# One step of a hybrid decoder layer on one core: in the last of a tile's four attention units, one product with a broadcast reciprocal in the place of two scalings by a column

## The chip, the core and the metric

The kernel runs on one core of a Trainium2 chip. The metric is the time of one execution on the device in microseconds (us); several executions of a kernel are measured and their median is given. The engines of the core are called here as the profile calls them: PE is TensorE (matrix products, with PEld for its weight loads), DVE is VectorE, ACT is ScalarE, POOL is GpSimd, and SP is SyncE, which here only issues transfers. Each engine works through its own instructions in the order in which they stand, and waits where a result of another engine is not there yet.

## The reference

One layer is computed for 2048 prompt tokens and 64 sampled tokens of width 1024: a normalised input goes through one projection, whose columns feed two groups of heads, a sliding-window attention and a gated linear attention (GLA); both outputs are joined, projected and added to the input, and a squared-ReLU MLP follows. The change is in the softmax of the sliding-window attention, cut here to what matters:

```python
def sink_softmax(scores, mask, sink):
    scores = jnp.where(mask, scores, -jnp.inf)
    m = jnp.maximum(jnp.max(scores, axis=-1, keepdims=True), sink)
    p = jnp.exp(scores - m)
    return p / (jnp.sum(p, axis=-1, keepdims=True) + jnp.exp(sink - m))

def swa_banded(q, k, v, sinks):
    # blocks of 128 queries, each against its own 128 keys and the 128 before
    ...
    p = sink_softmax(scores, mask, sink)
    out = jnp.einsum('bnhgqk,bnkhd->bnqhgd', p.astype(v.dtype), vv)
```

There are 8 query heads and 2 key heads, each 64 wide. Everything is float32 at the inputs and outputs; the kernel splits each operand of a large matrix product into a rounded high part and a remainder, and multiplies them in three passes.

## The kernel before

The kernel works in stages. The first (some 20 to 320 us of the profile) runs the sliding-window attention over 16 tiles of 128 prompt tokens, and beside it the input projection of later tiles. Then come the GLA with its own projection, the output projection, and the MLP, which takes the larger part of the time and is bound by PE.

**The attention of a tile** is cut into four units, `unit(i, r, jj, mo)` (L456), for tile `i`, key head `r` and pair of query heads `jj`, in the order (0,0), (0,1), (1,0), (1,1). A unit handles two query heads. Its steps, with the names that the profile uses:

- POOL copies the negated sinks into an extra column of the tile `s` (L464).
- PE computes the scores `sc` of both heads (128 queries by 256 keys each; 128 keys in tile 0).
- DVE adds the mask and takes the row minimum, writing `s` and `m` (the custom instruction and its accumulator read).
- ACT takes the exponential of `s` and sums it into `den`, a column for each head.
- DVE inverts `den` (RECIPROCAL, L487) and scales each head's half of `s` by its column of `den` (two TENSOR_SCALAR instructions, L489). `s` and `den` lie in SBUF, in float32.
- PE transposes the four 128x128 blocks of `s` into `pT`; ACT copies them rounded into `ph`; DVE takes the remainder `pl`.
- PE multiplies with the values into `av`, ACT copies one half to `rest`, and DVE adds both halves into `mo`.

Four units are in flight at different steps, so the engines find work of several units, of the projection (`proj`) and of the next tiles' preparation between them: the transposed input `xT`, split by ACT and DVE into `xh` and `xl`; and the transposed queries and keys `pq` and `pk`, split into `qh`, `ql`, `kh`, `kl` (L406).

**The rotary embedding** of a later tile runs on POOL (`rotate`, L379): two products into `tb` (L386, 320 elements per partition each), one product in place (L392), and two sums into `rot` (L395 with 512 and L401 with 128 elements). All of them read two operands from SBUF. Around them stand small copies on POOL: `kl` (L445, L440), `kh` (L435, L439) and the sinks (L464). In some tiles POOL also multiplies and splits weights of the GLA projection (L261, L263).

**What sets the order.** PE, ACT and DVE instructions of this stage go through `InOrder` (L120), which keeps the order in which the Python code issues them; POOL's and SP's are placed by the scheduler. In every tile, the scaling of unit (1,1) stands on DVE behind the split `qh` and that unit's reciprocal, and ahead of `mo`, the splits of `vv` and `glr`, and the mask step of the next tile's unit. As PE, ACT and DVE are called through this helper, their instructions of the stage carry the line L130 in the profile, and are told apart by the tiles that they write.

Of the kernel before, what the change touches and what calls it, by code (L numbers as in the profile page):

```python
# [16 lines left out]
ALU = mybir.AluOpType  # L17
# [4 lines left out]
P = 128  # L22
# [93 lines left out]
def f32(ap):  # L116
    return ap.bitcast(F32)
# [23 lines left out]
def hybrid_step_kernel(ctx: ExitStack, tc: tile.TileContext, I, O):  # L141
# [21 lines left out]
    te, ac, dv = (InOrder(tc, engine) for engine in (nc.tensor, nc.scalar, nc.vector))  # L163
# [4 lines left out]
    def bank(shape, kind, name):  # L168

        return ps.tile(shape, F32, tag=kind, name=name, bufs=1 if kind in "de" else 2)  # L170
# [285 lines left out]
    def unit(i, r, jj, mo):  # L456

        nkt = min(i + 1, 2)
        nk = nkt * P
        rr = half_of[r]  # L460
        u_ = f"{i}_{r}_{jj}"
        h0 = r * 4 + jj * 2
        s = sp.tile([P, 2, nk + 1], F32, tag="s", name=f"s_{u_}", bufs=3)
        nc.gpsimd.tensor_copy(s[:, :, nk : nk + 1], sink[:, h0 : h0 + 2].unsqueeze(2))  # L464
        yield
        qs, ks, kl = heads[i]
        kh, kl = (t[:, r].rearrange("p a k -> p (a k)")[:, 2 * P - nk :] for t in (ks, kl))
        sc = bank([P, 2, nk], "b", f"sc_{u_}")
        for u in range(2):
            j = jj * 2 + u  # L470
            te.matmul(sc[:, u, :], qs[r][:, j, :], kh, start=True, stop=False)
            te.matmul(sc[:, u, :], qs[r][:, j, :], kl, start=False, stop=True)
        yield
        m = sp.tile([P, 2], F32, tag="m", name=f"m_{u_}", bufs=3)
        for u in range(2):
            dv.tensor_tensor_reduce(
                s[:, u, :nk], sc[:, u, :], amask[:, 2 * P - nk :], scale=1.0,
                scalar=sink[:, h0 + u : h0 + u + 1], op0=ALU.add, op1=ALU.min, accum_out=m[:, u : u + 1],
            )
        yield  # L480
        den = sp.tile([P, 2], F32, tag="den", name=f"den_{u_}", bufs=3)
        for u in range(2):
            ac.activation(
                s[:, u, :], s[:, u, :], AF.Exp, scale=-1.0, bias=m[:, u : u + 1], accum_out=den[:, u : u + 1]
            )
        yield
        dv.reciprocal(den, den)  # L487
        for u in range(2):
            dv.tensor_scalar(s[:, u, :nk], s[:, u, :nk], den[:, u : u + 1], None, op0=ALU.mult)  # L489
        yield  # L490
        pT = bank([P, nkt, 2, P], "c", f"pT_{u_}")
        for u in range(2):
            for kt in range(nkt):
                te.transpose(pT[:, kt, u, :], s[:, u, kt * P : (kt + 1) * P], ident)
        yield
        ph = sp.tile([P, nkt, 2 * P], F32R, tag="ph", name=f"ph_{u_}", bufs=2)
        pl = sp.tile([P, nkt, 2 * P], F32R, tag="pl", name=f"pl_{u_}", bufs=2)
        pf = pT.rearrange("p k u q -> p k (u q)")
        ac.activation(ph, pf, AF.Copy)
        yield  # L500
        dv.tensor_tensor(pl, pf, f32(ph), op=ALU.subtract)
        yield
        av = bank([P, 2 * P], "e", f"av_{u_}")
        vs = [vals[t] for t in range(i + 1 - nkt, i + 1)]
        both, hi, lo = ([v[:, r, u] for v in vs] for u in (slice(2), 0, 1))
        both = [v.rearrange("p u d -> p (u d)") for v in both]
        out = mo[rr, jj * 2 : jj * 2 + 2].rearrange("p j q -> p (j q)")
        if nkt == 1:
            te.matmul(av[:HD], hi[0], ph[:, 0], start=True, stop=False)
            te.matmul(av[:HD], hi[0], pl[:, 0], start=False, stop=False)  # L510
            te.matmul(av[:HD], lo[0], ph[:, 0], start=False, stop=True)
            yield
            ac.activation(out, av[:HD], AF.Copy)
        else:
            te.matmul(av, both[0], ph[:, 0], start=True, stop=False)
            for kt in range(2):
                te.matmul(av[:HD], hi[kt], pl[:, kt], start=False, stop=False)
            te.matmul(av, both[1], ph[:, 1], start=False, stop=True)
            yield
            rest = sp.tile([P, 2 * P], F32, tag="spc", name=f"rest_{u_}", bufs=2)  # L520
            ac.activation(rest[:HD], av[HD:], AF.Copy)
            yield
            dv.tensor_tensor(out, av[:HD], rest[:HD], op=ALU.add)
        if (r, jj) == (1, 1):
            stores.append((mix_d[i][:, 0:4, :], mo))
        yield
# [240 lines left out]
    def units():  # L767
        for i in range(NB):
            mo = sp.tile([P, 4, P], F32, tag="mo", name=f"mo_{i}", bufs=2)
            for u in range(4):  # L770
                yield unit(i, u // 2, u % 2, mo)
        mo = sp.tile([P, 4, NS], F32, tag="mo", name="mo_s", bufs=2)
        for c in range(2):
            for r in range(2):
                yield sample_unit(c, r, cached, kcs, mo)
# [1312 lines left out]
```

## Time and profile before

| | |
|---|---|
| time, median of 3 runs | 2264.04 us (2259.86 to 2265.18) |
| the profiled execution's own time | 2263.19 us |
| its span, first to last instruction | 2261.4 us |
| PE busy | 2183.5 us (97% of the span), 11816 matrix products |
| DVE busy | 1529.9 us (68%) |
| ACT busy | 1221.4 us (54%) |
| POOL busy | 259.4 us (11%), nearly all in the first third |
| granted TensorE clock, mean | 0.995 |

A row of the timeline gives the start and the duration in us, the engine, the line, the operation, the tiles written and read, their shapes, and how many instructions of a kind are merged into the row (xN); a bracket at its end tells how long the engine had been idle before it and what it waited for. A row of the chain of waits gives the start, the length and the holder of one piece of the work that ended last. As instructions of one engine overlap a little in the records, the start of a row can lie a little ahead of the end of the one before it.

### The profile page before, as it was taken

To read this page: it belongs to the slowest core of one execution; us is meant where nothing else is said; L and a number is where in the kernel's file an instruction comes from. 1 tells how busy PE (TensorE), PEld (TensorE's weight loads), DVE (VectorE), ACT (ScalarE), POOL (GpSimd) and SP (SyncE) were. 2 spreads that over 40 slices of the span, in tenths; PEclk is the share of its full clock that TensorE was granted. 3 is DMA by queue.
4 is the path that set the end of the run, shared out by engine and by line. 5 is a ranking of instruction groups with operands and counts; after the bars stand their busy time and mean duration, and the time that the engine had idled before them with its cause. 6 is when DMAs were issued, how large, how long until landed. Compare 5 with 4: busy or idle time off the path is not lost.

```text
span 2261.4 us, 34140 instructions
## 1 busy us (share of the span) xinstructions
PE 2183.5 (97%) x11816; PEld 1868.7 (83%) x11816; DVE 1529.9 (68%) x3102; ACT 1221.4 (54%) x2594; POOL 259.4 (11%) x417
## 2 busy tenths in 40 slices
PE   8999999999999999999999999999999999999998
PEld 7888888999998887788888788887888888788876
DVE  5888877776765565777788664447676666455566
ACT  5778766556664444555545564334544454454444
POOL 3566422111111110000000000000000000000000
PEclk9999999999999999999999999999999999999999
DMA  6334322214335558967777885557644443766675
GB/s 231 119 133 143 102 90 82 67 57 148 126 122 196 184 181 312 313 222 243 251 254 253 284 290 181 180 167 231 195 179 154 154 154 140 252 201 198 192 241 169
DMA packets 237256, 417.81 MB, mean 185 GB/s; under 512 B 25172, under 2 KB 137276, under 8 KB 232972
## 3 DMA queue, kind: packets, MB, share of 16 engines
q1 hardware_dynamic: 237084, 415.64, 54.8%
q8 instruction: 93, 1.52, 0.3%
q14 instruction: 79, 0.65, 0.1%
HBM read 268.44 MB, written 148.18 MB: 184 GB/s over the span
## 4 chain that ended last, share of the span: by engine, by line
PE 64%; DVE 15%; ACT 8%; DMA 8%; issue 3%; POOL 1%; SPq 0%; DVEq 0%; ACTq 0%; POOLq 0%
PE dn L130 21%; PE uc L130 6%; PE ua L130 6%; PE out L1250 6%; PE gproj L130 5%; PE ud L130 3%; PE ue L130 3%; PE ub L130 3%; DMA rt<-t_d 3%; DVE s L130 2%; PE proj L130 2%; PE dsam L130 1%; DVE pl L130 1%; PE o L130 1%; PE sam L130 1%
## 5 line engine op out<-in xcount | busy, mean ns | idle before, releaser
L130 PE MATMUL dn<-o0t,o0s 128*128 128x512 f32 x896 | 350.7, 391 | 9.0 <-ACT o0t L218 8.8
L130 PE MATMUL dn<-o1t,o0s 128*128 128x512 f32 x896 | 351.3, 392 | 3.1 <-DVE o1t L219 3.1
L130 PE MATMUL dn<-o0t,o1s 128*128 128x512 f32 x896 | 349.9, 391 | 0.0
L219 DVE TENSOR_TENSOR o1s<-rs,o0s 128x512 fp32r<-128x512 f32 x224 | 154.6, 691 | 197.2 <-ACT o0s L218 182.8
L218 ACT ACTIVATE o0s<-rs 128x512 fp32r<-128x512 f32 x224 | 141.1, 630 | 249.9 <-PE dn L130 206.0
L130 PE MATMUL gproj<-wg,gx 128*128 128x384 f32 x1408 | 268.5, 343 | 0.1
L130 PEld LDWEIGHTS gproj<-wg,gx 128*128 128x128 f32 x1408 | 241.6, 189 | 4.5 <-issue 4.3
L130 ACT ACTIVATE st<-st 128x512 f32<-128x512 f32 x224 | 141.1, 630 | 158.9 <-DVE st L130 154.9
L130 PEld LDWEIGHTS dn<-o0t,o0s 128*128 128x128 f32 x896 | 168.6, 188 | 48.9 <-ACT o0t L218 11.9
L130 PEld LDWEIGHTS dn<-o1t,o0s 128*128 128x128 f32 x896 | 168.5, 188 | 43.7 <-DVE o1t L219 7.9
L130 PEld LDWEIGHTS dn<-o0t,o1s 128*128 128x128 f32 x896 | 168.5, 188 | 35.0
L219 DVE TENSOR_TENSOR o1t<-rt,o0t 128x512 fp32r<-128x512 f32 x224 | 153.9, 687 | 64.3 <-ACT o0t L218 63.9
L218 ACT ACTIVATE o0t<-rt 128x512 fp32r<-128x512 f32 x224 | 139.6, 624 | 91.7 <-DMA rt<-t_d 70.0
L130 PE MATMUL uc<-H,s 128*128 128x512 f32 x768 | 186.7, 391 | 0.0
L130 PE MATMUL ua<-H,w 128*128 128x512 f32 x744 | 179.2, 390 | 0.0
L130 PEld LDWEIGHTS uc<-H,s 128*128 128x128 f32 x768 | 144.1, 188 | 31.9
L130 PEld LDWEIGHTS ua<-H,w 128*128 128x128 f32 x744 | 138.7, 188 | 28.2
L1250 PE MATMUL out<-wo,mt 128*128 128x512 f32 x680 | 158.9, 392 | 1.9 <-ACT mt L218 1.8
L1250 PEld LDWEIGHTS out<-wo,mt 128*128 128x128 f32 x680 | 126.5, 188 | 28.6 <-ACT mt L218 2.1
L208 POOL TENSOR_TENSOR frs<-rs_v,half 128x1 f32<-128x1 f32 (+1 forms) x13 | 8.4, 657 | 1230.2 <-DVE rs_v L206 1230.2
L130 DVE TENSOR_TENSOR st<-st 128x512 f32<-128x512 f32 x160 | 110.7, 692 | 35.1 <-ACT st L130 31.8
L130 ACT ACTIVATE s<-t 128x1024 fp32r<-128x1024 f32 x62 | 65.8, 1061 | 93.5 <-PE ud L130 29.0
(388 smaller groups left out, 4231.2 us busy)
## 6 DMA issues: line engine op xcount, KB each, us to landing
s_d<-st SPq DMA_DIRECT2D x32, 1792.0 KB, 7.6
rs<-s_d SPq DMA_DIRECT2D x224, 256.0 KB, 2.9
raw<-in_w_up SPq DMA_DIRECT2D x64, 512.0 KB, 5.2
rt<-t_d SPq DMA_DIRECT2D x128, 256.0 KB, 3.3
rt<-in_w_down SPq DMA_DIRECT2D x96, 256.0 KB, 2.8
t<-in_w_down SPq DMA_DIRECT2D x64, 256.0 KB, 3.7
t_d<-t SPq DMA_DIRECT2D x32, 512.0 KB, 6.6
gx<-xt_d SPq DMA_DIRECT2D x28, 512.0 KB, 4.8
```

Source lines behind the costliest of these rows:

```text
L130: ins = call(*a, **k)
L208: nc.gpsimd.tensor_tensor(out, v[:n], e, op=ALU.pow)
L218: nc.scalar.activation(hi, src, AF.Copy)
L219: vector.tensor_tensor(lo, src, f32(hi), op=ALU.subtract)
L1250: te.matmul(banks[c], x, w[:, c * 512 : (c + 1) * 512], start=k + u == 0, stop=k == KT - 1 and u == len(products) - 1,)
```

## The change

In the last of a tile's four units, (r, jj) = (1, 1), the two TENSOR_SCALAR instructions are replaced by one TENSOR_TENSOR product over both heads. Its second operand is `den`, broadcast along the keys (each of its two columns is read 256 times, or 128 times in tile 0). The other three units stay as they were. Each element is multiplied by the same factor as before.

```diff
         dv.reciprocal(den, den)
-        for u in range(2):
-            dv.tensor_scalar(s[:, u, :nk], s[:, u, :nk], den[:, u : u + 1], None, op0=ALU.mult)
+        if (r, jj) == (1, 1):
+            dv.tensor_tensor(
+                s[:, :, :nk], s[:, :, :nk], den.unsqueeze(2).to_broadcast([P, 2, nk]), op=ALU.mult
+            )
+        else:
+            for u in range(2):
+                dv.tensor_scalar(s[:, u, :nk], s[:, u, :nk], den[:, u : u + 1], None, op0=ALU.mult)
         yield
```

In the built program, 32 TENSOR_SCALAR instructions give way to 16 TENSOR_TENSOR instructions at the same places on DVE. Every other instruction of every engine stands where it stood.

## The prediction

> **What bounds the kernel now.** The page has PE busy for 97% of the span, so an edit on DVE can pay only where PE waits. I therefore read the busy time by stage first. The row of the attention stage (its window, the length, then busy time and instructions of PE, PEld, DVE, ACT and POOL, the granted clock, the DMA share and GB/s):
>
> ```profile
> 53.00:300.00 247.00, 231.81 (x1524) 212.15 (x1525) 214.51 (x630) 188.91 (x520) 143.12 (x256) 1.00 0.36 124
> ```
>
> PE is busy 231.81 of 247 us at the full clock: 15 us of waits lie here, and the change is in this stage alone. Next the chain of waits over one tile of it, from one scaling of unit (1,1) to the next:
>
> ```profile
> 141.56 1.51 DVE s L130 x2
> ...
> 145.79 0.69 DVE ql L130
> ...
> 159.07 1.51 DVE s L130 x2
> ```
>
> The chain runs on DVE alone from the first row past `ql` to the splits of the next tile, then over PE and ACT, and back to the scaling. A tile takes 159.07 - 141.56 = 17.51 us, and the 1.51 us pair that the change replaces is a link of this loop. Why 1.51? The timeline of DVE and POOL, in windows so narrow that single instructions show:
>
> ```profile
> 141.56 0.64 DVE L130 TENSOR_SCALAR s<-s,den 128x256 f32<-128x256 f32 x1
> 142.12 0.95 DVE L130 TENSOR_SCALAR s<-s,den 128x256 f32<-128x256 f32 x1
> 141.18 0.87 POOL L386 TENSOR_TENSOR tb<-qk,rope 128x320 f32<-128x320 f32 x1
> 142.01 0.91 POOL L386 TENSOR_TENSOR tb<-qk,rope 128x320 f32<-128x320 f32 x1
> ```
>
> The first scaling ends at 142.20, 0.15 after the first rotary product (142.05); the second at 143.07, 0.15 after the second (142.92). Each waits out one POOL instruction and needs 0.15 us more. Where in the stage does this recur? Three rows of DVE's timeline, for the tiles 0, 14 and 15:
>
> ```profile
> 53.02 1.56 DVE L130 TENSOR_SCALAR s<-s,den 128x128 f32<-128x128 f32 x2
> 298.01 1.44 DVE L130 TENSOR_SCALAR s<-s,den 128x256 f32<-128x256 f32 x2
> 314.29 0.62 DVE L130 TENSOR_SCALAR s<-s,den 128x256 f32<-128x256 f32 x2
> ```
>
> The first two are the first and the last of 15 such collisions, one in each tile. In tile 15 POOL rotates nothing any more, and the pair takes 0.62: its undisturbed price.
>
> **The change part by part.** *The product by itself.* The trace has a product of that size, both operands in SBUF and one of them broadcast, in the GLA stage:
>
> ```profile
> L1118 DVE TENSOR_TENSOR qd<-qz,dec 128x512 f32<-128x512 f32 x14 | 9.6, 686 | 0.0
> ```
>
> 0.69 us against 0.62: where POOL is idle, the change costs 0.07. (The Trainium skill, "VectorE: DVE Perf Modes", section "The perf-mode tier table", speaks against the change in the same way: a float32 scaling out of SBUF runs at the double rate, a two-tensor product at the single one. By that rule alone 16 units would cost 16 x 0.07 = 1.1 us. The trace agrees on the undisturbed prices, but not that they decide, since the pair takes 1.51 here.)
>
> *Does the product wait for POOL too?* Products with both operands in SBUF do, in the GLA stage:
>
> ```profile
> 372.37 1.29 POOL L959 TENSOR_TENSOR s_sg<-s_sg,gp_s 64x512 f32<-64x512 f32 x1 [7.23 <-ACT s_sg L958]
> 373.74 1.27 POOL L961 TENSOR_TENSOR s_sg<-s_sg,ggla 64x512 f32<-64x512 f32 x1
> 372.66 1.15 DVE L1014 TENSOR_TENSOR after<-after,before 128x128 f32<-128x128 f32 x1
> 373.85 1.31 DVE L1015 TENSOR_TENSOR before<-before 128x128 f32<-128x128 f32 x1
> 509.90 1.29 POOL L959 TENSOR_TENSOR sg<-sg,gp 128x512 f32<-128x512 f32 x1 [5.12 <-ACT sg L958]
> 511.27 1.35 POOL L961 TENSOR_TENSOR sg<-sg,ggla 128x512 f32<-128x512 f32 x1
> 510.74 0.73 DVE L1026 SCALAR_TENSOR_TENSOR pr<-gp 128x256 f32<-128x256 f32 x1 [1.05 <-ACT gp L613]
> ```
>
> L1014 ends at 373.81, 0.15 after L959 (373.66), so it got in ahead of the L961 behind it. L1015, issued just after L961 began, sits that one out and ends at 375.16, 0.15 after it. L1026, twice as long, ends 0.28 after its POOL product (511.47 against 511.19). So what is left after the release is about 0.13 us per 128 elements, 0.55 for 512 (an estimate from these rows; its upper bound is the full 0.69 of L1118). The new product is issued at 141.56 as the pair is now, waits until 142.05, gets in ahead of the second rotary product as the first scaling does today, and ends at 142.60. On DVE that gains 143.07 - 142.60 = 0.47 us: one wait in the place of two.
>
> *What POOL pays.* The second rotary product must let the new one pass. Behind today's 0.15 us it took 0.91 instead of 0.87, and L961 behind a pass of 0.28 took 1.35 instead of 1.27 above. So the delay is at least this 0.04 and at most the whole pass of 0.55. I take 0.40, near the upper end, since a pass of 0.15 already costs something and the rest should count in full. POOL's next instructions move by it:
>
> ```profile
> 144.63 1.29 POOL L395 TENSOR_TENSOR rot<-qk,tb 128x512 f32<-128x512 f32 x1
> 145.88 0.46 POOL L401 TENSOR_TENSOR rot<-qk,tb 128x128 f32<-128x128 f32 x1
> 146.88 0.44 POOL L440 CAST kl<-kl 128x256 fp32r<-128x256 f32 x1
> 148.23 0.19 POOL L464 COPY s<-sink 128x2 f32<-128x2 f32 x1 [0.91 <-ACT wg L130]
> ```
>
> *Does the gain pass on?* PE transposes `s` in two steps today, the first as soon as one head is scaled. Afterwards all four blocks wait for the product.
>
> ```profile
> 143.21 0.41 PE L130 MATMUL pT<-ident,s 128*128 128x128 f32 x2 [0.46 <-DVE s L130]
> 143.38 0.43 PE L130 MATMUL proj<-wa_hi,xl 128*128 128x392 f32 x1
> 146.54 0.42 PEld L130 LDWEIGHTS xT<-ident,x 128*128 128x128 f32 x4 [0.45 <-DVE ql L130]
> 147.50 0.60 PE L130 MATMUL pT<-ident,s 128*128 128x128 f32 x4
> 147.86 0.42 PE L130 MATMUL proj<-wa_hi,xh 128*128 128x392 f32 x1
> 143.72 0.60 ACT L130 ACTIVATE ph<-pT 128x512 fp32r<-128x512 f32 x1 [1.23 <-PE pT L130]
> 144.75 0.68 DVE L130 TENSOR_TENSOR pl<-pT,ph 128x512 fp32r<-128x512 f32 x1
> ```
>
> Today the second step starts 0.14 after the scaling, so `pT` would start at 142.74. Four in a row let `proj` start 0.36 later (147.50 to 147.86), at 143.10 instead of 143.38: PE gains only 0.28 here. But it idles 0.45 us before `xT`, where it waits for `ql` on DVE, and the missing 0.19 fits into that. `pT` ends at 143.34 and `ph`, 0.10 later as now, runs to 144.04, ahead of `pl` (144.28 by DVE's own pace). So nothing holds DVE up, and `ql`, `xT` and what follows start 0.47 earlier.
>
> *The next pair*, of unit (0,0), is issued at 146.72 today and ends 0.16 after L440, at 147.48. It moves to 146.25. There the delayed L395 ends at 146.32 and the delayed L401 at 146.74, with 0.04 for letting a scaling in at 146.78, so its second scaling ends at 146.93, 0.55 earlier: by the phase slightly more than 0.47. POOL ends L440 near 147.73, and the sink copy of the last row can still start near 147.76, 0.47 earlier than now; what follows it is not on the chain. I take 0.55 a tile.
>
> *The sum.* Twelve tiles (1, 2 and 4 to 13) at 0.55 give 6.6. Three others differ:
>
> ```profile
> 57.41 0.91 DVE L130 TENSOR_SCALAR s<-s,den 128x256 f32<-128x256 f32 x2
> 110.20 0.43 POOL L440 CAST kl<-kl 128x256 fp32r<-128x256 f32 x1
> 111.54 0.19 POOL L464 COPY s<-sink 128x2 f32<-128x2 f32 x1 [0.90 <-PE pT L130]
> 112.54 0.53 ACT L130 ACTIVATE wg<-wg_raw 128x384 fp32r<-128x384 f32 x1 [1.40 <-POOL wg_raw L261]
> 302.26 0.46 POOL L401 TENSOR_TENSOR rot<-qk,tb 64x128 f32<-64x128 f32 x1
> 302.85 0.65 DVE L130 TENSOR_SCALAR s<-s,den 128x256 f32<-128x256 f32 x2
> ```
>
> In tile 3 the sink copy is followed by weight products that ACT waits for; with L440 ending some 0.45 later, near 111.08, the copy starts near 111.12: 0.42. In tile 0 the pair at 57.41 already waits for POOL's `rot`, which comes no earlier: 0. In tile 14 the pair that ends at 303.50 moves to 302.38 and meets L401, delayed to 302.66 to 303.12, so it ends near 303.26: 0.24. Tile 15 loses 0.07. Together 6.6 + 0.42 + 0 + 0.24 - 0.07 = 7.2 us. Behind the attention only the start moves. The profiled execution goes from 2263.19 (its span of 2261.4 and 1.8 around it) to 2256.0; it lies 0.85 under the median of 2264.04, so against the median the forecast is **2256.8 us**.
>
> **The rivals.** (a) *The product does not wait for POOL.* It ends at 141.56 + 0.69 = 142.25, the tile gains 0.82, 14 tiles 11.5 and tile 0 some 0.6: 2252. For it: `pl` above, a product too, takes 0.68 beside a busy L395. Against it: `pl` reads one operand from PSUM; L1014 and L1015 read both from SBUF and wait.
>
> (b) *PE or POOL sets the pace.* If only PE's 0.28 passes on: 14 x 0.28 = 3.9, so 2260. For it: POOL's slack is nearly used up. Against it: the 0.45 idle before `xT`.
>
> (c) *The second rotary product goes first.* The new product waits until 142.92 and ends at 143.47, 0.40 later than the pair today; 14 tiles make 5.6: 2269.6, slower than before. It decides from the point at which POOL's second product, queued without a gap (142.01 against 142.05), takes its turn ahead of the waiting DVE instruction. Against it: the first scaling wins that turn today. (The Trainium skill, "SBUF — State Buffer", section "Who interferes with whom", has issue order decide, with the loser blocked for the whole instruction; by that the product, issued first, goes first and the sum is the forecast's. L1014 at 0.15 and L1015 at 0.15 after their POOL products agree.)
>
> (d) *It waits for a run of POOL instructions*, through the rotation's third product as well:
>
> ```profile
> 142.99 1.56 POOL L392 TENSOR_TENSOR qk<-qk,rope 128x640 f32<-128x640 f32 x1
> ```
>
> That one ends at 144.55, so the product would end at 145.1, 2.0 later than now, 28 us in 14 tiles: 2292. No row shows a DVE instruction passed over twice.
>
> **How the numbers follow.** Forecast 0.72, (a) 0.10, (b) 0.06, (c) 0.06, (d) 0.06. A measurement here tells 0.3% (6.8 us, the line at 2257.2) from no change. The forecast lies just past that line, and the runs of before spread over 5.3 us, so it falls short of it in some 28 of 100 cases. Faster: 0.72 x 0.72 + 0.10 = 0.62. Within 0.3%: 0.20 + 0.06 + 0.06 = 0.32, with (b) and (c). Slower: (d), 0.06. The forecast's own range, 0.3 to 0.75 a tile, is 2253.5 to 2260.5; with (a), (b) and the spread of the runs it becomes 2251 to 2264.
>
> **What would show it.** Right: unit (1,1)'s scaling as one TENSOR_TENSOR of some 1.05 us that ends 0.55 after the first L386; a second L386 of some 1.3; tiles of 16.95 us; the GLA stage starting some 7 us earlier, all later stages as long as before. A product of 0.69 beside L386 means (a), one of 1.9 means (c), an L386 pair still at 1.74 means that POOL pays nothing. The prediction is wrong if the product shortens as told and the tile keeps its 17.5 us: then another loop over PE, ACT or POOL is as long as this one.

## The result, and the profile after

| | before | the change |
|---|---|---|
| median (runs) | 2262.2 us (20 runs, 2257.31 to 2265.35) | 2256.9 us (20 runs, 2250.69 to 2262.71) |
| ratio to before, 95% interval | | 0.9977 (0.9968 to 0.9985) |
| span of the profiled execution | 2261.4 us | 2251.9 us |
| granted clock | 0.995 | 0.993 |
| first to last scaling of unit (1,1) | 53.02 to 314.29: 261.27 us | 53.11 to 309.33: 256.22 us |

The change is faster by 5.3 us, or 0.23%, with an interval of 0.15 to 0.32%. The forecast of 2256.8 stands beside a median of 2256.9, but that is luck: it was counted from a median of three runs of before, 1.8 us above the one of twenty, and the forecast gain was 7.2 us, 1.9 more than the measured one. The two errors cancel. The same kernel measured again later gave 2255.76 against 2261.2, ratio 0.9977 (0.9967 to 0.9987). The gain is real, as both intervals lie below 1, and most probably a little smaller than the 0.3% that was set as the line between faster and no change. The prediction had given 0.62 to a gain past that line and 0.32 to a time within it; what came is within it.

The two spans differ by 9.5 us, but from the first to the last scaling of unit (1,1) the difference is 5.05. The rest lies in stages that hold the same instructions in both kernels, and is spread from one execution to the next: from the start of the last scaling to the end it is 1947.1 us in before and 1942.6 in the change, and between 1941.7 (e8) and 1947.6 (e11) in the profiles of the experiments below. I therefore read tiles rather than spans.

The chain of waits of the change, one tile (start, length, holder):

```profile
157.00 1.04 DVE s L130
...
160.76 0.69 DVE ql L130
...
161.68 0.10 DVE s L130
161.78 0.49 issue
162.27 0.34 DVE s L130
...
174.20 1.04 DVE s L130
```

The link of 1.51 us is now one of 1.04, and the tile takes 174.20 - 157.00 = 17.20 us in the place of 17.51. The chain runs through the same work as before. The product and its neighbours on POOL, from the timeline of the change in narrow windows, first in this tile, then in tiles 14 and 15:

```profile
157.00 1.04 DVE L130 TENSOR_TENSOR s<-s,den 128x512 f32<-128x512 f32 x1
156.62 2.14 POOL L386 TENSOR_TENSOR tb<-qk,rope 128x320 f32<-128x320 f32 x2
156.62 0.87 POOL L386 TENSOR_TENSOR tb<-qk,rope 128x320 f32<-128x320 f32 x1
157.45 1.31 POOL L386 TENSOR_TENSOR tb<-qk,rope 128x320 f32<-128x320 f32 x1
...
293.23 0.97 DVE L130 TENSOR_TENSOR s<-s,den 128x512 f32<-128x512 f32 x1
309.33 0.69 DVE L130 TENSOR_TENSOR s<-s,den 128x512 f32<-128x512 f32 x1
```

The second L386 starts at 157.45 and takes 1.31 us in the place of 0.91. The product gets in ahead of it and ends at 158.04, 0.55 after the first L386 (156.62 + 0.87 = 157.49). In tile 15, where POOL rotates nothing, the product takes 0.69.

The surprise lies in unit (0,0), whose two scalings were not touched. In the kernel before, its pair took 0.76, in the prediction's tile:

```profile
146.72 0.76 DVE L130 TENSOR_SCALAR s<-s,den 128x256 f32<-128x256 f32 x2
```

Two tiles of the change, the first the one above, the second tile 5:

```profile
161.68 0.67 DVE L130 TENSOR_SCALAR s<-s,den 128x256 f32<-128x256 f32 x1
161.68 0.93 DVE L130 TENSOR_SCALAR s<-s,den 128x256 f32<-128x256 f32 x2
160.49 1.30 POOL L395 TENSOR_TENSOR rot<-qk,tb 128x512 f32<-128x512 f32 x1
161.73 0.47 POOL L401 TENSOR_TENSOR rot<-qk,tb 128x128 f32<-128x128 f32 x1
...
127.39 0.35 DVE L130 TENSOR_SCALAR s<-s,den 128x256 f32<-128x256 f32 x1
127.39 0.82 DVE L130 TENSOR_SCALAR s<-s,den 128x256 f32<-128x256 f32 x2
126.20 1.29 POOL L395 TENSOR_TENSOR rot<-qk,tb 128x512 f32<-128x512 f32 x1
127.44 0.62 POOL L401 TENSOR_TENSOR rot<-qk,tb 128x128 f32<-128x128 f32 x1
```

In both tiles the pair is issued some 0.10 us before L395 ends (161.68 against 161.79, 127.39 against 127.49). In tile 5 the first scaling gets in between L395 and L401 and ends at 127.74, 0.25 after L395. L401 is stretched from 0.46 to 0.62, and the pair takes 0.82. In the other tile the first scaling is passed over: it ends at 162.35, 0.15 after the end of L401 at 162.20, and the pair takes 0.93.

PE behind the product, from the timeline of the change:

```profile
158.18 0.63 PE L130 MATMUL pT<-ident,s 128*128 128x128 f32 x4 [0.56 <-DVE s L130]
158.56 0.43 PE L130 MATMUL proj<-wa_hi,xl 128*128 128x392 f32 x1
```

`pT` starts 0.14 after the product's end, and `proj` 0.38 after `pT`. What PE waits for in this stage, all tiles together (us in total, times, longest), in the kernel before:

```profile
PE pT L130 <- DVE s L130: 8.5, 23, 0.5
```

And in the change, with the busy time of the stage (columns as in the first row of the prediction) behind it:

```profile
PE pT L130 <- DVE s L130: 7.6, 14, 0.6
```

```profile
53.00:300.00 247.00, 233.71 (x1555) 217.66 (x1556) 214.60 (x631) 192.50 (x529) 154.08 (x261) 1.00 0.37 124
```

The waits are fewer, but 7.6 us remain: half a microsecond a tile is left on this path. In the same 247 us PE has 233.71 us of work where it had 231.81, and POOL is busy 154.08 where it was 143.12: the longer second L386 makes 14 x 0.40 = 5.6 of that. The rest is smaller: five more of POOL's instructions fall into the window (261 against 256), since the tiles come earlier, and others, L401 among them, take longer.

### The profile page after: what moved, and what is told of

It reads as the page before. It is cut to its first block, busy times and chain, and to the rows that moved or that the text cites. A ratio compares the mean times of both kernels' runs of the same rounds, so it can differ in the third digit from the quotient of the medians.

```text
span 2251.9 us, 34109 instructions
## 1 busy us (share of the span) xinstructions
PE 2182.2 (97%) x11816; PEld 1872.9 (83%) x11816; DVE 1526.4 (68%) x3086; ACT 1222.8 (54%) x2594; POOL 266.8 (12%) x417
## 4 chain that ended last, share of the span: by engine, by line
PE 71%; DVE 12%; ACT 7%; DMA 6%; issue 2%; POOL 1%; SPq 0%; DVEq 0%; ACTq 0%; POOLq 0%
PE dn L130 23%; PE uc L130 7%; PE ua L130 7%; PE out L1255 6%; PE gproj L130 5%; PE ue L130 4%; PE ub L130 4%; PE ud L130 4%; PE proj L130 2%; DMA rt<-t_d 2%; DVE s L130 2%; PE sam L130 1%; PE dsam L130 1%; PE o L130 1%; DVE pl L130 1%
```

## The experiments

Eleven runs; all but the repetition are variants of the kernel before. Times are medians, ratios are to before in the same comparison.

| run | what differs from before | time | ratio (95%) | (1,1) | (0,0) | tile |
|---|---|---|---|---|---|---|
| e1 | (1,1) product, reciprocal in the score bank | 2251.43 | 0.9951 (0.9939 to 0.9964) | 0.69 | 0.62 | 16.88 |
| e2 | e1, and (0,0) likewise | 2252.94 | 0.9955 (0.9943 to 0.9968) | 0.69 | 0.69 | 16.88 |
| e3 | (1,1) as two products, SBUF | 2267.85 | 1.0024 (1.0015 to 1.0033) | 1.77 | 0.76 | 17.77 |
| e4 | the change, (0,0) product with score bank | 2251.74 | 0.9953 (0.9939 to 0.9966) | 1.03 | 0.69 | 16.97 |
| e5 | (1,1) product, reciprocal in an `av` bank | 2258.98 | 0.9989 (0.998 to 0.9998) | 0.69 | 0.92 | 17.41 |
| e6 | e5, and (0,0) likewise | 2261.43 | 1.0006 (0.9997 to 1.0014) | 0.69 | 0.69 | 17.45 |
| e7 | (1,1) product, reciprocal in the `pT` bank | 2248.65 | 0.994 (0.9928 to 0.9952) | 0.69 | 0.82 | 16.63 |
| e8 | e7, and (0,0) likewise | 2243.06 | 0.992 (0.9907 to 0.9934) | 0.69 | 0.69 | 16.50 |
| e9 | the change again | 2255.76 | 0.9977 (0.9967 to 0.9987) | 1.03 | 0.92 | 17.20 |
| e10 | pairs kept, their reciprocal in the `pT` bank | 2261.3 | 0.9998 (0.9989 to 1.0006) | 1.61 | 0.76 | 17.51 |
| e11 | the change, (0,0) likewise, SBUF | 2252.8 | 0.9972 (0.9961 to 0.9982) | 1.03 | 0.69 | 16.97 |

The last three columns are us in most of the tiles 4 to 11 of the profiled execution: the duration of the scaling in the two units, and the length of a tile.

**Is it the wait for POOL? (e1, e2)** The product stays, its reciprocal is written to PSUM, so that only one of the two operands lies in SBUF; the bank is that of the unit's own scores, which are used up by then (the edit against the change, in unit (1,1)).

```diff
-            dv.reciprocal(den, den)
+            rec = sc[:, 0, :2]
+            dv.reciprocal(rec, den)
             dv.tensor_tensor(
-                s[:, :, :nk], s[:, :, :nk], den.unsqueeze(2).to_broadcast([P, 2, nk]), op=ALU.mult
+                s[:, :, :nk], s[:, :, :nk], rec.unsqueeze(2).to_broadcast([P, 2, nk]), op=ALU.mult
             )
```

Expected of e1, and of e2, which does the same in unit (0,0):

> Unit (1,1) scaled by one product as in the change, but the reciprocal of den is written to the used-up score bank in PSUM, so that the product reads only one operand from SBUF. Theory (a product waits for POOL only where both operands lie in SBUF; the price is the turn that it must wait for): the product takes 0.69 us instead of 1.03, ends 0.82 earlier than the pair of before, the two L386 go back from 2.14 to 1.75 us, a tile takes 16.6 to 16.8 us instead of 17.20 (the change) and 17.51 (before), the time is some 11 us under before, near 2251. Rival (the gain of the change is that of one instruction fewer, wherever den lies): product 1.03, L386 2.14, tile 17.2, time as with the change, 2257.

> As before this one, and unit (0,0) is scaled in the same way, by one product with the reciprocal in PSUM. Theory: neither unit waits for POOL any more, both products take 0.69 us, a tile takes 16.5 to 16.65 us, the time is some 13 us under before, near 2249. Rival (by then another loop, over PE or ACT, is as long as DVE's): the products take 0.69 but the tile stays at 16.7 or more.

DVE, POOL and PE of e1 in one tile:

```profile
171.72 0.69 DVE L130 TENSOR_TENSOR s<-s,sc 128x512 f32<-128x512 f32 x1
171.46 1.69 POOL L386 TENSOR_TENSOR tb<-qk,rope 128x320 f32<-128x320 f32 x2
172.56 0.35 PE L130 MATMUL sc<-kh,qh 128*128 128x256 f32 x1 [0.91 <-DVE s L130]
```

And PE's waits over the stage of e1:

```profile
PE sc L130 <- DVE s L130: 13.4, 15, 1.0
```

The product takes its undisturbed 0.69 in the middle of the L386 pair, and POOL pays nothing (1.69). The wait for POOL was the price, and an operand in PSUM takes it away. The tile of 16.88 is worse than expected: the rows of PE have the reason, a new wait. The next scores need the bank, and PE now waits for the product's end to get it (13.4 us in 15 waits over the stage). In e2 the same wait (13.3 us in 15) holds the tile at 16.88, where 16.5 to 16.65 was expected, so a better (0,0) brings nothing; 16.7 or more is what the rival of that expectation had.

**One instruction or two? (e3)** The scalings of unit (1,1) become two products, a head each, both operands in SBUF (the edit against before, in that unit).

```diff
-            dv.tensor_scalar(s[:, u, :nk], s[:, u, :nk], den[:, u : u + 1], None, op0=ALU.mult)
+            dv.tensor_tensor(s[:, u, :nk], s[:, u, :nk], den[:, u : u + 1].to_broadcast([P, nk]), op=ALU.mult)
```

> Unit (1,1) scaled by two products, one for each head, both operands in SBUF. Theory (each instruction pays a turn behind POOL, and a product's pass is twice as long as a scaling's): the first ends 0.28 after the first L386, the second 0.28 after the second L386, which is itself some 0.15 later: together near 1.8 us instead of 1.51, tile 17.6 to 17.8 us, time 2 to 5 us over before. Rival (a product gets past POOL more easily than a scaling, whatever their number): together 1.2 us or less, tile 17.3 or less, time under before.

The timelines of DVE and POOL in e3:

```profile
162.08 0.77 DVE L130 TENSOR_TENSOR s<-s,den 128x256 f32<-128x256 f32 x1
162.77 1.08 DVE L130 TENSOR_TENSOR s<-s,den 128x256 f32<-128x256 f32 x1
161.70 0.87 POOL L386 TENSOR_TENSOR tb<-qk,rope 128x320 f32<-128x320 f32 x1
162.52 1.04 POOL L386 TENSOR_TENSOR tb<-qk,rope 128x320 f32<-128x320 f32 x1
```

Each waits one POOL instruction out and ends some 0.28 after it: 1.77 together, a tile of 17.77, and the kernel is 0.24% slower than before. That is 6.0 us, more than the 2 to 5 expected; tile 0, which takes 18.57 where it took 16.88, makes 1.7 of it. The product as an operation brings nothing; one turn in the place of two is what pays.

**Is unit (0,0) what is missing? (e4, e11)** Both keep the change in (1,1). e4 takes (0,0) off POOL by the score bank, e11 scales it by a product in SBUF as well. The edit of e4 against the change:

```diff
-        dv.reciprocal(den, den)
-        if (r, jj) == (1, 1):
+        rec = sc[:, 0, :2] if (r, jj) == (0, 0) else den
+        dv.reciprocal(rec, den)
+        if r == jj:
             dv.tensor_tensor(
-                s[:, :, :nk], s[:, :, :nk], den.unsqueeze(2).to_broadcast([P, 2, nk]), op=ALU.mult
+                s[:, :, :nk], s[:, :, :nk], rec.unsqueeze(2).to_broadcast([P, 2, nk]), op=ALU.mult
             )
```

In e11 only the condition changes, to `r == jj`, and `den` serves both units.

> The change as it is for unit (1,1), and unit (0,0) scaled by one product with the reciprocal in PSUM. Theory (the 0.25 us a tile that the change did not bring are spent by the pair of unit (0,0) behind L395 and L401): the product of (1,1) keeps 1.03, that of (0,0) takes 0.69 instead of 0.93, a tile takes 16.95 us instead of 17.20, the time is some 7.5 us under before, near 2254.5. Rival (PE's two-step transposes, or POOL's lateness, hold the tile up): tile 17.2, time as with the change, 2257.

> The change as it is (reciprocal in SBUF), done in unit (0,0) too. By the rule that a product in SBUF waits one POOL instruction out and then needs 0.55 us: in (0,0) it is issued a little before L395 ends and ends 0.55 after L395 if it wins that turn, or 0.55 after L401 if it loses it, as the first scaling does in most tiles of the change. Won: some 0.7 to 0.75 us in (0,0), tile 16.95 to 17.05, time 2250 to 2254. Lost: 0.10 + 0.45 + 0.55 = 1.1 us, tile 17.35 to 17.45, time 2258 to 2260.

Unit (0,0) in e11, on DVE and POOL:

```profile
161.31 0.69 DVE L130 TENSOR_TENSOR s<-s,den 128x512 f32<-128x512 f32 x1
160.13 1.28 POOL L395 TENSOR_TENSOR rot<-qk,tb 128x512 f32<-128x512 f32 x1
161.38 0.95 POOL L401 TENSOR_TENSOR rot<-qk,tb 128x128 f32<-128x128 f32 x1
```

With a (0,0) of 0.69 us the tile is 16.97 in both, the forecast's 16.95, while (1,1) still takes 1.03. So the missing part of a tile's gain lay in unit (0,0) and nowhere else. (The time of e4, 10.1 us under before, is better than the 7.5 expected of it; why is not known. That of e11, 7.8 under before, is as expected.) In e11 the product is issued 0.10 before L395 ends, as the scalings are, but it won that turn in all tiles from 2 to 13: it delays L401 to 0.95 and ends 0.59 after L395.

**Another bank (e5, e6).** The reciprocal goes to an unused half of the previous unit's `av` bank, to avoid the wait of the next scores; in e5 for (1,1), in e6 for (0,0) too.

```diff
-        av = bank([P, 2 * P], "e", f"av_{u_}")
+        avs.append(bank([P, 4 * P], "e", f"av_{u_}"))
+        av = avs[-1][:, : 2 * P]
...
+            rec = avs[-1][:, 2 * P : 2 * P + 2]
+            dv.reciprocal(rec, den)
```

> Unit (1,1) scaled by one product with the reciprocal in PSUM, now in the unused half of the bank of the previous unit's av instead of the score bank, which PE was waiting for. Theory (the tile of 16.88 us of the two kernels with the score bank was held up by PE's 0.91 us wait for that bank): no such wait, product 0.69, L386 pair some 1.7, a tile of 16.7 to 16.8 us with the pair of (0,0) waiting for L401, time near 2250. Rival (with the product at 0.69 another loop of PE or ACT is the bound at 16.88): tile 16.88, time 2251 to 2252.

> As the one before, and unit (0,0) in the same way. Theory: both products take 0.69 us and wait for nothing, a tile takes 16.6 us, the time is near 2248.5, the lowest of all. Rival (another loop is the bound): tile as in the run before, time as there.

Both missed. The product takes 0.69, but the reciprocal ahead of it now waits (e5, timeline of DVE):

```profile
193.85 0.17 DVE L130 RECIPROCAL av<-den 128x2 f32<-128x2 f32 x1 [0.59 <-ACT rest L130]
194.06 0.69 DVE L130 TENSOR_TENSOR s<-s,av 128x512 f32<-128x512 f32 x1
```

ACT reads the other half of that bank for `rest`, and the write waits for it. One wait has been traded for another, and the tile is 17.41.

**A bank that nobody needs meanwhile (e7, e8, e9).** The bank for this unit's own `pT` is taken a step earlier, and the reciprocal lies in its first two columns. PE's transposes into it need the finished product anyway. e7 does it for (1,1), e8 for (0,0) too.

```diff
+        pT = bank([P, nkt, 2, P], "c", f"pT_{u_}")
...
+            rec = pT[:, 0, 0, :2]
+            dv.reciprocal(rec, den)
...
         yield
-        pT = bank([P, nkt, 2, P], "c", f"pT_{u_}")
```

> The product of unit (1,1) with its reciprocal in the bank of this unit's own pT, which PE does not write before the product has ended, and which the softmax leaves alone otherwise. My theory (only a product with both operands in SBUF takes turns with POOL; the 0.36 us a tile that the version with the reciprocal in the score bank lost went to PE's wait for that bank): product 0.69 us, the pair of L386 near 1.69, no wait of the next unit's sc for the product, tiles of 16.6 to 16.8 us instead of 16.88, time 2248 to 2251. Rival: the next loop (ql, xT, the pair of unit (0,0)) is the limit at 16.88 whatever the bank: then the tile stays at 16.9 and the time at that of the score-bank version, 2251 to 2252, and the wait of sc is only replaced by another.

> The same with the product in unit (0,0) too. My theory: both products 0.69 us; the pair of unit (0,0) that this replaces was 0.62 where the first product already stood off POOL, so nothing more is gained unless the pair meets L395 or L401 again at its new place: tiles equal to those of the version with (1,1) alone if its pair is 0.62, up to 0.25 shorter if it is 0.93; time 2247 to 2251. Rival: as there, 16.9 a tile and 2251 to 2252.

> The change itself, beside the two versions above on one chip: 2255 to 2258, tiles of 17.20 us by my theory (the pair of unit (0,0) still loses its turn at the end of L395 in most tiles). Should the tiles be 16.95 this time, the lost turn was an accident of one execution and not of the kernel.

e7 came out as expected: 2248.65, tiles of 16.63 where (0,0) takes 0.82. e9 repeats the change; the first scaling of (0,0) loses its turn again in more than half of the tiles. e8 is better than its expectation by 4 us: 2243.06, in the same comparison 12.7 us below the change and 18.1 below before. Its unit (0,0) on DVE and POOL, then the waits of PE for the transposes and the busy time of its stage (columns as before):

```profile
157.21 0.69 DVE L130 TENSOR_TENSOR s<-s,pT 128x512 f32<-128x512 f32 x1
156.04 1.28 POOL L395 TENSOR_TENSOR rot<-qk,tb 128x512 f32<-128x512 f32 x1
157.28 0.46 POOL L401 TENSOR_TENSOR rot<-qk,tb 128x128 f32<-128x128 f32 x1
```

```profile
PE pT L130 <- DVE s L130: 0.5, 1, 0.5
```

```profile
52.50:299.50 247.00, 241.97 (x1615) 226.20 (x1616) 212.80 (x639) 199.34 (x550) 146.66 (x261) 1.00 0.38 128
```

DVE and POOL work side by side at full pace. PE waits for `s` once in the place of 23 times, and is busy for 241.97 of 247 us where it was 231.81: the stage is now nearly bound by PE. From the first to the last scaling of (1,1) e8 takes 247.03 us, 14.24 less than before, and its first scaling comes 0.55 earlier. The median gains 18.1, and the ratio's interval begins at 0.66%, or 14.9 us; the attention stage does not account for the rest, and single executions differ by up to 6 us behind it.

**The operation or the operand? (e10)** The pairs of scalings stay, their column moves into the `pT` bank.

> In units (0,0) and (1,1) the two scalings stay as before, and only their reciprocal column moves into the bank of pT. This parts the operand's place from the operation. My theory is that what takes turns with POOL is an operation whose large operands both lie in SBUF, or that runs at the double rate; a column of two numbers in PSUM changes neither for the scalings: pair of (1,1) still about 1.5 us, tile 17.4 to 17.6 us, time within 0.2% of before (2258 to 2264). Rival: any operand in PSUM frees an instruction: then each scaling takes 0.35 to 0.42 us beside POOL, the pair of (1,1) 0.65 to 0.75, the tile some 16.5 us, and the time is that of the two-product version with the reciprocal in pT's bank, 2243 to 2247; the single product would then add nothing of its own.

One tile of e10, DVE and POOL:

```profile
178.95 0.76 DVE L130 TENSOR_SCALAR s<-s,pT 128x256 f32<-128x256 f32 x1
179.63 0.94 DVE L130 TENSOR_SCALAR s<-s,pT 128x256 f32<-128x256 f32 x1
178.69 1.74 POOL L386 TENSOR_TENSOR tb<-qk,rope 128x320 f32<-128x320 f32 x2
```

Both scalings still wait, 1.63 us together, the tile stays at 17.51 and the time at that of before. (The profiled execution also has a tile 0 of 18.56 where before had 16.88, which the median does not show.) So an operand in PSUM frees the product and not the scaling. The rival, that any operand in PSUM frees an instruction, falls. (The Trainium skill, "SBUF — State Buffer", section "Who interferes with whom", parts them in this way: a DVE instruction with at most one SBUF input does not contend with GpSimd, unless it runs in a mode that uses both ports for one tensor. The product at 0.69 in e1, e7 and e8 and the scalings at 1.63 here agree, provided that the scalings run in such a mode. No run shows the mode itself; with POOL out of the way the pair takes 0.63 in tile 15 of e10, less than the product.)

## Why the prediction was right, and where it was off

*The bound.* Right. The loop ran over DVE's scalings, and a shortening of them came through to the tile wherever it brought no new wait (e4, e7, e11), until PE was nearly full (e8). In e1, e2, e5 and e6 a new wait took a part or all of it.

*The price of the collision.* Right. The pair cost two turns; e3, with two products, costs two turns as well.

*The product waits for POOL for one turn, and ends 0.55 after the first L386.* Right: 1.04 against 1.05 forecast, in 14 tiles 0.97 to 1.04. DVE's gain of 0.47 there was right as well: it is 1.51 - 1.04. Rivals (a), no wait, (c), the second rotary product goes first, and (d), a run of POOL instructions, each wanted another duration (0.69, 1.9 or 3.5) and are refuted by this row. That the wait for POOL is what separates 1.04 from 0.69 is shown by e1.

*POOL pays 0.40.* Right: the second L386 takes 1.31 in the place of 0.91. One of the rows behind this estimate was misread, without effect: the L961 of 1.27 was no undisturbed one, as L1014 had got in ahead of it.

*The gain passes PE.* Right. From the start of (1,1)'s scaling to that of (0,0)'s it was 146.72 - 141.56 = 5.16 us; it is 161.68 - 157.00 = 4.68, 0.48 less.

*The next pair.* Here the prediction failed. It let the first scaling of (0,0) slip in behind L395, L401 be delayed by 0.04, and the second scaling end 0.68 after the pair's start, which made 0.55 a tile of the 0.47. Two things were wrong:

- Where the first scaling does get in, L401 pays 0.16 (0.62 against 0.46) and not the 0.04 that was read from L386. That 0.04 belongs to a scaling that ends 0.15 after POOL's first instruction. Here it was issued only 0.10 ahead, had most of its own 0.35 us still to do, and ends 0.25 after L395. The pair takes 0.82, and the tile gains 0.42 (17.51 to 17.09 in e9, tile 1 of the change 17.50 to 17.08).
- Being issued some 0.10 before the end of L395, it often does not get in. Then the pair takes 0.93, and the tile gains 0.31 (17.51 to 17.20).

Worked into the sum: the twelve tiles gain 0.35 on average (4.14 together, from the starts of (1,1)'s scaling in both profiles) and not 0.55, so 2.5 us less. e4 and e11 show that this is the whole of what is missing in these tiles: with 0.69 in (0,0) the tile is 16.97.

*The other tiles.* Tile 3 gained 0.36 (0.42 forecast), tile 14 0.19 (0.24). Tile 3 is no confirmation: in e9, the same kernel, it took 20.31 us, 1.13 more than in before, while the twelve tiles gained 4.21 there. Tile 0 gained 0.37 where nothing was forecast: the chain of before there runs from `xT` over ACT's `xh` and DVE's `xl`, not through the pair that waits for `rot`, so the step that stopped the gain was not on the path. Together: 4.14 + 0.36 + 0.19 + 0.37 = 5.06, and 5.05 is what lies between the first and the last scaling by the rows. Less 0.07 in tile 15, the sum is 4.99 against 5.3 measured.

*The range.* Its two ends count different tiles: 2253.5 lies 14 tiles at 0.75 us below the 2264.04 of before, 2260.5 only 12 at 0.3. With 14 the upper end would be 2259.8; the measured time lies inside either way.

*Rival (b), PE or POOL sets the pace*, wanted 2260. The gain is in fact between that of (b), 3.9 us, and that of the forecast, but not for the reason that (b) gives: tiles of 16.97 (e11) and of 16.50 (e8) run with the same PE work and the same POOL work.

## What to carry to other kernels

When DVE and POOL run side by side, read their timelines in narrow windows and look for a DVE instruction that ends a fixed time after a POOL one: here a scaling 0.15 us, a product over 512 elements 0.55 us. Then count turns rather than instructions: one long product (1.04) beat two short scalings (1.51) although it is the dearer one alone (0.69 against 0.62). Better than fewer turns is none: a product whose small operand lies in a PSUM bank that nobody needs meanwhile ran at its full pace, and which bank is chosen decides whether a new wait eats the gain (16.88, 17.41 and 16.63 us a tile with unit (1,1) alone, in e1, e5 and e7). And after each shortening, work out at which moment the next instruction on that engine now falls: here a few hundredths of a us decided a turn.

## What the runs showed of the hardware that was not expected

**When a turn is decided.** I counted, in eight profiles (before, the change twice, e3, e5, e7, e10, e11), the scalings and products of `s` with both large operands in SBUF that were issued while POOL was in L395 with L401 behind it, or in the first L386 with the second behind it, and before that next one was recorded as started. The lead is the POOL instruction's end less the start of the DVE instruction; won means that DVE got in before the next POOL instruction.

| lead, us | scaling: won / lost | product: won / lost |
|---|---|---|
| 0.082 to 0.093 | 0 / 8 | 1 / 0 |
| 0.095 to 0.103 | 6 / 13 | 8 / 0 |
| 0.104 to 0.129 | 14 / 0 | 4 / 0 |
| 0.154 and more | 37 / 0 | 62 / 0 |

So to be issued first was not enough for a scaling: it had to be some 0.10 us ahead, though it started before the POOL instruction behind it in every one of these cases. The product won at 0.091 to 0.103, where most scalings lost. (The Trainium skill, "SBUF — State Buffer", section "Who interferes with whom", has issue order decide; the runs agree from a lead of 0.104 on, and below that not for scalings.) Why the two differ, and whether products have a limit of their own further down, stays open.

**What the passed instruction pays** is what the DVE instruction has left when POOL's first one ends, less some 0.10 us. A scaling that ended 0.15 after it cost the second L386 0.04 (0.91 against 0.87); one that ended 0.25 after it cost L401 0.16 (0.62 against 0.46). A product that ended 0.55 after it cost L386 0.44 (1.31 against 0.87), and one that ended 0.59 after it cost L401 0.49 (0.95). In all cases of the table that were won against L401, it ended 0.31 to 0.33 after the DVE instruction, and in those won against L386, that ended 0.71 to 0.73 after it. So a late lead costs twice: below some 0.10 the turn can be lost, and a little above it POOL pays more for a short instruction.

**A gain beside the product.** In e7 the tile is 16.63 where (0,0) takes 0.82, against 17.09 in e9: 0.46 less, of which the product explains 0.34 (1.03 to 0.69). Its reciprocal is recorded ahead of the end of `qh`:

```profile
171.54 0.68 DVE L130 SCALAR_TENSOR_TENSOR qh<-pq,qh 64x512 fp32r<-64x512 f32 x1
172.15 0.15 DVE L130 RECIPROCAL pT<-den 128x2 f32<-128x2 f32 x1
172.34 0.69 DVE L130 TENSOR_TENSOR s<-s,pT 128x512 f32<-128x512 f32 x1
```

It starts 0.07 before `qh` ends; the one that writes `den` starts 0.02 after (292.32 + 0.69 = 293.01 and 293.03, in the rows of the change at the end). From the start of `qh` to that of the product it is 0.80 here and 0.91 in the change (293.23 - 292.32), which is 0.11 of the remaining 0.12. e10 has the earlier start too, with the scalings waiting that much longer. An output in PSUM is not enough for it: in e8 the reciprocal of unit (0,0) goes to `pT` as well, but stands behind `ql`, and starts 0.03 after `ql` has ended (156.97, the first two rows below). In the kernel, `qh` is filled in its upper half from its lower one at this point, and `ql` the other way round; whether that makes the difference was not tried.

```profile
156.28 0.69 DVE L130 SCALAR_TENSOR_TENSOR ql<-pq,ql 64x512 fp32r<-64x512 f32 x1
157.00 0.17 DVE L130 RECIPROCAL pT<-den 128x2 f32<-128x2 f32 x1
...
292.32 0.69 DVE L130 SCALAR_TENSOR_TENSOR qh<-pq,qh 64x512 fp32r<-64x512 f32 x1
293.03 0.17 DVE L130 RECIPROCAL den<-den 128x2 f32<-128x2 f32 x1
```
